# A hybrid attention and pooling layer: x loaded by tiles of tokens, scaled there and turned on TensorE, and the index queries projected in two lines

## The chip, the cores and the metric

The kernel runs on one core of one Trainium2 chip. The metric is device time in microseconds (us) of one execution; three executions of the kernel before took 515.8, 517.5 and 519.13 us, median 517.5. The core has five engines with a queue of instructions each, worked off in order: PE (TensorE, matrix products; PEld is its loading of stationary operands), DVE (VectorE), ACT (ScalarE), POOL (GpSimd) and SP, which here only issues transfers between main memory and SBUF.

## The reference, cut to what matters

One decoder layer for 1024 tokens of width 1024. The part that the change touches is the beginning:

```
mod = silu(c) @ w_ada + b_ada;  shift, scale, gate = split(mod, 3)
h = rms_norm(x, norm_w) * (1 + scale) + shift      # rms over a token's 1024 values
proj = h @ w_in                                    # w_in has 2888 columns
u_pool, g_pool, q, k, v, g_attn, qi, ki, wi = split(proj)
```

Behind it: a pooling mixer on `u_pool`; keys, queries and index queries with rotary positions; for every token the 256 keys with the best index score (computed from `qi`, `ki`, `wi`); attention over these; both branches gated and projected by `w_out`, times `gate`, added to x. Tokens below 256 take all their keys, so index queries are needed for tokens 256 to 1023 only.

## The kernel before, in words

All products are made with operands split in a high part (fp32r) and the rest: h is held as `hhi` and `hlo`, a weight as `wh` and `wl`, and a product is the three matmuls hhi·wh, hhi·wl, hlo·wh. h lies with its 1024 channels in 8 blocks j of 128 partitions and the tokens along the row.

The order of the instructions is not written out. Pieces of the work are generators ("strands") that yield operations; the class `Flow` (lines 302 to 402) keeps an estimated clock for each engine and, while the program is built, issues the operation that could start first, shifted by a number for each strand out of the table `EARLY` (line 38). `Either` (line 272) picks one of several engines for an operation in the same way. What results is a fixed queue for each engine. Every op is issued at line 228, so all rows of the profile carry L228.

**The lead** is what happens up to the first 61 us:

- `token_sums` (line 515) loads x transposed (`xT`, channels on partitions) in 8 blocks of 512 KB, the last two in halves, squares them on ACT, adds them on DVE, and sums over channels on PE by 48 one-column matmuls with a vector of ones. `token_scales` turns the 1024 roots into a row that is broadcast to all partitions (`rsb`).
- `modulations` (line 626) makes scale and shift of block j on DVE: two instructions over 128x1024, one for each of the two 512 KB tiles `wa` that `lead_loads` fetches; `gear` and `shift` finish the 128 values.
- `h_block` (line 687; `first_block` for j = 0): xn = x·rsb on POOL, then `hhi` and the shifted xn on ACT, and `hlo` on DVE or POOL, all over 1024 tokens.
- `query_loads` and `weight_splits` load the weights of the index queries (`wq`, four tiles of 512 KB in a ring `ld` of two) and split them, high part on ACT, rest on POOL.
- `lead_line` (line 737) projects the index queries for all 8 blocks j: for each j three products for tokens 512 to 1023 (4 matmuls of 512 columns each) and three for tokens 256 to 511 (4 of 256 columns), one after the other. It holds 6 of the 8 banks of PSUM, the other two hold silu(c), which `modulations` reads.

Then `main_line` begins: `key_value_rows` (the matmuls m<-wkh,hhi of 328 columns), gates, queries and the pooling mixer in the sequence `ORDER`, with the index scores, the selection and the attention on DVE, ACT and POOL beside it.

Of the kernel before, what the change touches and what calls it, by code (L numbers as in the profile page):

```python
# [7 lines left out]
F32 = mybir.dt.float32  # L8
F32R = mybir.dt.float32r
# [18 lines left out]
ORDER = "a0 a2 a1 q1 q2 | q0 m1 q3 m2 m3 m0 a3"  # L28
# [9 lines left out]
EARLY = {"main": 0.6, "fill": 0.4, "weights": 0.0, "evac": -1.0, "side": 0.2, "first": -0.4, "h": -0.2,  # L38
         "mods": -0.2, "select": -0.1, "scores": -0.6, "attend": -1.1, "late": 1.0, "kv": -0.3, "qi": -0.8,
         "pick": -0.6, "mix": -0.33, "rotated": 0.23, "query_loads": -0.28, "exps": -0.11, "score_sums": -1.07,  # L40
         "key_value_out": -0.93, "index_queries": -0.86, "norm": -0.46, "gate_loads": -1.2, "token_scales": -3.22,
         "gate_mods": -0.39, "unit": -1.06, "index_scores": -0.91, "lead_loads": 0.74, "out": -1.53,
         "lead_out": -1.24, "weight_loads": 0.51, "key_value_weights": 0.67, "main_line": 0.66, "output_line": 0.91,
         "turns": -1.46, "finish": -1.64, "index_keys": -1.47, "h_block": 0.28, "attention_keys": -0.36,
         "turned": -1.0, "h_blocks": -0.59, "gated": -2.15, "modulations": -0.09, "low": 0.65, "gear": -0.51,
         "attention": -0.86, "maxima": -0.99, "score_relus": -0.67, "gated 7": -1.82, "gated 3": -1.0,
# [5 lines left out]
         "exps 5": -0.25, "key_value_out 4": -3.2, "query_norms": 0.27, "exps 8": 0.04, "key_value_out 5": -1.22,  # L52
# [6 lines left out]
         "shift 6": -1.88, "key_value_out 6": -2.24, "norm 1": -2.54, "gear 4": 0.99, "products": -1.29,  # L59
         "shift 4": -0.32, "norm 5": -1.64, "low 1": -2.52, "turns 6": -2.43, "gated 6": -2.43, "turns 8": -1.76,  # L60
         "h_block 3": 0.04, "shift": 0.2, "gear 8": -2.5, "lead_line": 1.29, "gear 7": -1.58,
         "index_queries 3": -3.45, "index_queries 1": -2.08, "lead_splits": -0.3, "shift 5": -0.05,
         "first_block": -2.64, "shift 2": 0.74, "lead_out 1": -1.22, "shift 8": 1.3, "out 7": -0.3, "unit 3": -1.17,
         "turns 3": -2.02, "key_value_out 1": -2.25, "exps 4": -0.27, "mix 2": -0.25, "exps 2": 0.46, "out 6": -0.73,
         "gated 8": -2.42, "out 5": -1.79}
# [5 lines left out]
SAFE = {"side": 1.0, "unit": 0, "query_norms": 0, "h_block": 0.59, "rotated": 0.48, "query_loads": 0,  # L71
        "norm": 0.29, "weight_loads": 1.12, "key_value_out": 0.39, "turned": 0.26, "finish": 0, "index_keys": 0.85,
        "main_line": 0, "output_line": 0, "gate_mods": 1.06, "selection": 0, "low": 0.27, "maxima": 0,
        "attention": 0.44, "lead_out": 0, "score_relus": 0, "lead_loads": 0.28, "score_sums": 0.18, "mix": 0.96,
        "main": 0, "modulations": 0.09, "out": 0.39, "turns": 0.34, "exps": 0, "lead_line": 0.6, "shift": 0,
        "token_scales": 0.08, "index_scores": 0.19, "products": 0, "index_queries": 0.34, "attend": 0,
        "weight_splits": 0}

SCALED = (7,)

SUMS = (1, 4,)

WKM = 6
# [3 lines left out]
PHOP = -0.148  # L87
STT = 0.079
# [6 lines left out]
PW_POOL = 0.088  # L95
XO_POOL = 0.108
# [10 lines left out]
MIX = 4  # L107
# [6 lines left out]
WA_AHEAD = 3  # L114
# [13 lines left out]
class Op:  # L128
# [85 lines left out]
    def issue(self, flow):  # L214
# [8 lines left out]
        if self.eng == "ACT":  # L223
            table = TABLES.get(self.args[2] if len(self.args) > 2 else None)
            if table and table != flow.table:
                flow.table = table
                us += 1.3
        self.fn(*self.args, **self.kw)  # L228
# [180 lines left out]
def hybrid_layer(ctx, tc, xT, cT, nwT, badaT, wada, wq, wet, wkv, qnw, knw, wpool,  # L409
# [71 lines left out]
    ones = const([P, 1], F32)  # L481
# [32 lines left out]
    xt, hhi, hlo, wk = [], {}, {}, []  # L514
    tab = {}

    def token_sums():
# [3 lines left out]
        halves = [slice(512, 1024), slice(0, 512)]  # L521
        pieces = [(j, slice(0, 1024)) for j in range(6)] + [(j, c) for c in halves for j in (6, 7)]
        for j, c in pieces:
            if len(xt) == j:
                xt.append((yield big(s="xt")))
            yield SP.dma_start(xt[j][:, c], xT[j][:, c])
            if j == 0:
# [3 lines left out]
        yield G.memset(ones, 1.0)  # L531
# [19 lines left out]
        tab["sums"] = []  # L551
        for _ in range(2):
            tab["sums"].append((yield bank(4)))
        started = set()

        def sums(t, c, last):
            for h, half in enumerate(halves):
                if half.start >= c.start and half.stop <= c.stop:
                    for b in range(4):
                        o = half.start + b * P  # L560
                        yield mm(tab["sums"][h][:, b:b + 1], t[:, o:o + P], ones, h not in started, last and b == 3)
                        started.add(h)

        sq, acc = {}, None
        for j, c in pieces:
            if j not in sq:
                sq[j] = yield big(s="sq")
            yield A.activation(sq[j][:, c], xt[j][:, c], AF.Square)
            if j in SUMS:
                yield from sums(sq[j], c, False)  # L570
            elif acc is None:
                acc = sq[j]
                continue
            else:
                yield V.tensor_tensor(acc[:, c], acc[:, c], sq[j][:, c], op=OP.add)
                if j == NT - 1:
                    yield from sums(acc, c, True)
            if c.start == 0:
                flow.drop(sq[j])
        flow.drop(acc)  # L580

    def token_scales():
        rsb = yield big(s="rsb")
# [1041 lines left out]
```

## Time and profile before

| | us |
|---|---|
| three executions | 515.8, 519.13, 517.5 (median 517.5) |
| the profiled execution | 518.54, of which the span of the instructions is 516.8 |
| PE busy | 491.5 (95% of the span) |
| DVE, ACT, POOL busy | 417.1 (81%), 385.1 (75%), 149.5 (29%) |
| first matmul of the lead line | 23.51 |
| first matmul of the keys and values | 61.20 |

Times in the profile count from the start of the span. A group of the trace such as "43.59 1.09 PE ... x4" began at 43.59, and its four pipelined matmuls were busy for 1.09; what a group costs in a sequence is the distance to the start of the next one. "[0.83 <-DMA xt<-xT]" behind a row is the time that the engine sat idle before it, and what ended the wait.

### The profile page before, as it was taken

The numbers are of one execution on the slowest core, as the hardware profiler recorded it, in microseconds if no ns is written. First come the engines' busy times: TensorE is split into PE (matmuls) and PEld (weight loads), VectorE is DVE, ScalarE is ACT, GpSimd is POOL, SyncE is SP. The second block draws the span as 40 slices with busy tenths as digits, with TensorE's granted clock in tenths as the row PEclk, the third lists the DMA queues.
The fourth block names the chain that finished last, engine by engine and source line by source line (L and its number), as shares of the span: only waits on it lengthen the run. The fifth ranks groups of instructions, "written<-read, shape, count | busy, mean of one in ns | idle before, by whom it ended". The sixth has DMA issues, their size and how long they took to land.

```text
span 516.8 us, 8355 instructions
## 1 busy us (share of the span) xinstructions
PE 491.5 (95%) x2840; PEld 369.3 (71%) x2840; DVE 417.1 (81%) x890; ACT 385.1 (75%) x875; POOL 149.5 (29%) x166
## 2 busy tenths in 40 slices
PE   4899999999999989999999999999999999898996
PEld 4788899766768857878878776886664658453484
DVE  1799897799689799989999999778979995675342
ACT  6589433697778999999837999799898747669410
POOL 1399310001001133567033247524521222200000
PEclk9999999999999999999999998999999999999999
DMA  8996613011205112111120014575532135501054
GB/s 300 402 409 217 227 42 122 22 45 38 75 10 184 41 42 81 42 41 42 41 81 22 21 63 125 160 246 164 183 103 63 42 101 192 156 1 41 1 190 136
DMA packets 28171, 58.35 MB, mean 113 GB/s; under 512 B 3808, under 2 KB 7904, under 8 KB 28128
## 3 DMA queue, kind: packets, MB, share of 16 engines
q1 hardware_dynamic: 28128, 57.81, 33.2%
q8 instruction: 22, 0.36, 0.3%
q14 instruction: 21, 0.17, 0.1%
HBM read 47.32 MB, written 10.49 MB: 112 GB/s over the span
## 4 chain that ended last, share of the span: by engine, by line
PE 51%; DVE 24%; issue 7%; ACT 7%; POOL 4%; DMA 2%; DVEq 0%; SPq 0%; POOLq 0%; ACTq 0%
PE m L228 51%; DVE junk L228 7%; DVE selw L228 3%; ACT ex L228 3%; DVE ex L228 2%; POOL wl L228 1%; DVE nx L228 1%; DMA xo<-y_d 1%; DVE xq L228 1%; DVE wa L228 1%; ACT hhi L228 1%; DVE gp L228 1%; ACT ajunk L228 1%; DVE u L228 1%; POOL xn L228 1%
## 5 line engine op out<-in xcount | busy, mean ns | idle before, releaser
L228 PE MATMUL m<-hhi,wh 128*128 128x512 f32 (+1 forms) x320 | 120.9, 400 | 0.3 <-ACT hhi L228 0.3
L228 PE MATMUL m<-hhi,wl 128*128 128x512 f32 (+1 forms) x320 | 115.5, 383 | 0.0
L228 PE MATMUL m<-hlo,wh 128*128 128x512 f32 (+1 forms) x320 | 114.0, 381 | 0.5 <-DVE hlo L228 0.2
L228 ACT ACTIVATE ajunk<-key,xq 128x768 bf16<-128x768 uint16 (+2 forms) x93 | 96.3, 1036 | 1.3
L228 POOL TENSOR_TENSOR wl<-ld,wh 128x512 fp32r<-128x512 f32 x40 | 59.5, 1491 | 45.3 <-ACT wh L228 26.7
L228 PEld LDWEIGHTS m<-hhi,wh 128*128 128x128 f32 x320 | 59.7, 192 | 16.6 <-issue 4.1
L228 DVE TENSOR_SCALAR_CACHE_REDUCE junk<-key,xq 128x384 bf16<-128x384 uint16 (+2 forms) x93 | 69.1, 743 | 2.1
L228 PEld LDWEIGHTS m<-hhi,wl 128*128 128x128 f32 x320 | 59.6, 191 | 12.2 <-issue 1.4
L228 PEld LDWEIGHTS m<-hlo,wh 128*128 128x128 f32 x320 | 58.6, 188 | 13.0 <-DVE hlo L228 0.9
L228 ACT ACTIVATE ex<-ex,mx,c 128x384 f32<-128x384 f32 (+7 forms) x64 | 54.9, 859 | 5.1 <-DVE mx L228 5.0
L228 ACT ACTIVATE kt<-m 128x512 f32<-128x512 f32 (+1 forms) x80 | 37.7, 525 | 11.0 <-PE m L228 5.4
L228 DVE SCALAR_TENSOR_TENSOR score<-kt,c,score 128x1024 f32<-128x1024 f32 (+5 forms) x42 | 39.9, 951 | 7.3 <-ACT kt L228 5.5
L228 PE MATMUL m<-kT,qr 64*128 64x512 f32 (+3 forms) x192 | 40.6, 512 | 1.7 <-DVE mx L228 1.3
L228 DVE CUSTOM_DVE_ANT_0 ex<-m,key 128x512 f32<-128x512 f32 (+1 forms) x48 | 30.9, 662 | 7.2 <-PE m L228 7.0
L228 DVE SCALAR_TENSOR_TENSOR xo<-m,c,xo 128x512 f32<-128x512 f32 x23 | 17.2, 749 | 23.1 <-PE m L228 15.4
L228 PE MATMUL m<-pw,vrow 128*64 128x512 f32 x144 | 33.1, 599 | 0.1
L228 PEld LDWEIGHTS m<-kT,qr 64*128 64x128 f32 x192 | 19.4, 188 | 18.3 <-issue 11.0
L228 ACT CAST wh<-ld 128x512 fp32r<-128x512 f32 x33 | 20.3, 624 | 15.7 <-PE m L228 11.4
L228 POOL TENSOR_SCALAR_AFFINE_SELECT score<-score 128x128 f32<-128x128 f32 x6 | 3.8, 633 | 88.0 <-DVE score L228 80.8
L228 ACT COPY pw<-m 128x512 f32<-128x512 f32 x51 | 26.3, 610 | 3.9 <-PE m L228 3.9
L228 PEld LDWEIGHTS m<-c,ex 64*128 64x128 f32 x576 | 21.3, 139 | 10.0 <-ACT ex L228 3.2
L228 POOL TENSOR_SCALAR wh<-ld 128x512 fp32r<-128x512 f32 x23 | 17.7, 770 | 37.1 <-PE m L228 36.3
(193 smaller groups left out, 1062.5 us busy)
## 6 DMA issues: line engine op xcount, KB each, us to landing
wa<-wada SPq DMA_DIRECT2D x24, 512.0 KB, 7.5
ld<-wet SPq DMA_DIRECT2D x16, 512.0 KB, 3.4
ld<-wout SPq DMA_DIRECT2D x24, 256.0 KB, 3.0
xo<-xT SPq DMA_DIRECT2D x16, 256.0 KB, 3.8
y_d<-xo SPq DMA_DIRECT2D x16, 256.0 KB, 2.6
xo<-y_d SPq DMA_DIRECT2D x16, 256.0 KB, 3.0
outT<-xo SPq DMA_DIRECT2D x16, 256.0 KB, 2.3
xt<-xT SPq DMA_DIRECT2D x6, 512.0 KB, 7.3
```

Source lines behind the costliest of these rows:

```text
L228: self.fn(*self.args, **self.kw)
```

## The change

x is loaded with tokens on partitions (`xR`, 8 tiles of 128 tokens by 1024 channels), the tiles 7 to 4 (tokens 512 to 1023) first, and tiles 3 to 0 inside `lead_loads` before the `wa` tiles of block 2 (`XB = 2`). A token's sum of squares now comes along a row (`token_tile`: one instruction with accumulation on DVE or ACT), and its root scales the tile in place on DVE, POOL or ACT. `token_turns(n)` turns a half on PE: 64 transposes of 64 partitions by 128 channels for each half, in four groups q that fill two banks of PSUM each; `token_out` copies a bank to SBUF. The squares on PE, the sums on DVE and the row `rsb` are gone. `h_half` makes hhi and hlo for half a block (512 tokens). `lead_line` becomes two strands, one for tokens 512 to 1023 and one for 256 to 511, each over all 8 blocks; the weight chunks stay until both have used them. The loads of the key and value weights wait for the modulation of all 8 blocks (`WKM` 6 to 8), and `EARLY` has many new numbers. Behind the lead the work is the same; a few neighbours change places on DVE, POOL and PE, and q2 is projected before q1.

```diff
-ORDER = "a0 a2 a1 q1 q2 | q0 m1 q3 m2 m3 m0 a3"
+ORDER = "a0 a2 a1 q2 q1 | q0 m1 q3 m2 m3 m0 a3"
...
-         "gate_mods": -0.39, "unit": -1.06, "index_scores": -0.91, "lead_loads": 0.74, "out": -1.53,
+         "gate_mods": -0.39, "unit": -1.06, "index_scores": -0.91, "lead_loads": 1.12, "out": -1.01,
...
-WKM = 6
+COLD = 17.877
+
+XB = 2
+
+WKM = 8
...
+    def token_tile(st):
+
+        yield lambda: st in xr
+        t, r = xr[st], rs[:, st:st + 1]
+        sq = yield big(s="sq")
+        ways = [V.scalar_tensor_tensor(sq, t, 1.0, t, op0=OP.mult, op1=OP.mult, accum_out=r),
+                A.activation(sq, t, AF.Square, accum_out=r)]
+        yield Either(*ways) if st < 4 else ways[st == 4]
+        flow.drop(sq)
+        if st >= 4:
+            yield A.activation(r, r, AF.Sqrt, scale=1.0 / 1024.0, bias=eps_sb)
             yield V.reciprocal(r, r)
...
+                yield A.activation(rs[:, 0:4], rs[:, 0:4], AF.Sqrt, scale=1.0 / 1024.0, bias=eps_sb)
+                yield V.reciprocal(rs[:, 0:4], rs[:, 0:4])
+                rooted.append(st)
+            yield lambda: bool(rooted)
+        ways = [V.tensor_scalar(t, t, r, None, op0=OP.mult), G.tensor_scalar(t, t, r, 1.0, op0=OP.mult, op1=OP.mult),
+                A.activation(t, t, AF.Copy, scale=r)]
+        yield Either(*ways) if st < 4 else ways[st == 6]
+        token_scaled.append(st)
+
+    def token_turns(n):
+
+
+        toks = range(4 - 4 * n, 8 - 4 * n)
+        yield lambda: all(st in token_scaled for st in toks)
+        rows = slice(0, 64), slice(64, 128)
+        for q in range(NT // 2):
+            xt[q, n] = yield big(s="xt")
+            ps = []
+            for r in range(2):
+                ps.append((yield bank(keep=1 - r)))
+            yield Group([PE.transpose(ps[r][:, (j * 4 + b) * 64:(j * 4 + b + 1) * 64],
+                                      xr[st][rows[r], (2 * q + j) * P:(2 * q + j + 1) * P], ident[rows[r], rows[r]])
+                         for j in range(2) for b, st in enumerate(toks) for r in range(2)])
+            for r in range(2):
+                flow.spawn(token_out(q, n, r, ps[r]), "h")
+        flow.drop(*[xr[st] for st in toks])
...
     def lead_loads():
         for j in range(NT):
+            for st in (3, 2, 1, 0) if j == XB else ():
+                t = yield big(s="xr")
+                yield SP.dma_start(t, xR[st])
+                xr[st] = t
             yield lambda: len(modded) >= j - WA_AHEAD
...
+    def h_half(j, n, hi, lo):
+        c = halves[n]
+        x, g, m = xt[j // 2, n][:, j % 2 * 512:j % 2 * 512 + 512], gs[:, j:j + 1], mod_sb[:, j:j + 1]
+        yield Either(A.activation(hi[:, c], x, AF.Identity, scale=g, bias=m),
+                     V.tensor_scalar(hi[:, c], x, g, m, op0=OP.mult, op1=OP.add))
         hhi[j] = hi
...
+    def lead_line(c):
+        if c:
+            yield lambda: len(turned_in) == 2 * NT
+        p = (slice(512, 1024), slice(256, 512))[c]
```

In the rows below, xr_176, xr_173, xr_166 and xr_161 are the tiles of tokens 0 to 511, hhi_272 and hhi_293 are blocks 0 and 1, hhi_365 is block 2, hhi_401 block 3; c_76 is the identity matrix.

SP's queue around the second half of x, before (behind the last piece of x):

```order
L228 DMA wa_205<-wada 128x1024
L228 DMA wa_207<-wada 128x1024
L228 DMA ld_209<-wq 128x1024
L228 DMA wa_210<-wada 128x1024
L228 DMA wa_215<-wada 128x1024
L228 DMA wa_217<-wada 128x1024
L228 DMA wa_219<-wada 128x1024
```

and now (behind the first four tiles of x):

```order
L238 DMA wa_147<-wada 128x1024
L238 DMA wa_149<-wada 128x1024
L238 DMA ld_151<-wq 128x1024
L238 DMA wa_152<-wada 128x1024
L238 DMA wa_159<-wada 128x1024
L238 DMA xr_161<-xR 128x1024
L238 DMA xr_166<-xR 128x1024
L238 DMA xr_173<-xR 128x1024
L238 DMA xr_176<-xR 128x1024
L238 DMA wa_274<-wada 128x1024
```

Four tiles of x moved from ahead of the first `wa` to behind the `wa` of block 1; the last of them is the 13th transfer of 512 KB.

PE's queue in the lead, before, from the first block to the second:

```order
L228 MATMUL m<-hhi_253,wh_212 128x512 x4
L228 MATMUL m<-hhi_253,wl_213 128x512 x4
L228 MATMUL m<-hhi_253,wh_212 128x256 x4
L228 MATMUL m<-hhi_253,wl_213 128x256 x4
L228 MATMUL m<-hlo_254,wh_212 128x512 x4
L228 MATMUL m<-hlo_254,wh_212 128x256 x4
L228 MATMUL m<-hhi_302,wh_232 128x512 x4
```

and now, from the first product of the first block to the last of the second:

```order
L238 MATMUL m<-hhi_272,wh_154 128x512 x4
L238 MATMUL m<-hhi_272,wl_155 128x512 x4
L238 MATMUL m<-hlo_273,wh_154 128x512 x4
L238 MATMUL m<-hhi_293,wh_208 128x512 x4
L238 MATMUL m<-hhi_293,wl_209 128x512 x4
L238 MATMUL m<-c_76,xr_176 128x64 x2
L238 MATMUL m<-c_76,xr_173 128x64 x2
L238 MATMUL m<-c_76,xr_166 128x64 x2
L238 MATMUL m<-c_76,xr_161 128x64 x2
L238 MATMUL m<-c_76,xr_176 128x64 x2
L238 MATMUL m<-c_76,xr_173 128x64 x2
L238 MATMUL m<-c_76,xr_166 128x64 x2
```

Only five groups of matmuls stand ahead of the transposes of the second half; the products of blocks 2 to 7, the third product of block 1 and all products of 256 columns stand behind the first of them.

ACT's queue in the same place, now (sq are squares, xt the copies of turned x out of PSUM):

```order
L238 ACTIVATE sq_180,c_92<-xr_176 128x1024
L238 ACTIVATE c_92<-c_92,c_79 128x4
L238 ACTIVATE xr_161<-xr_161,c_92 128x1024
L238 ACTIVATE xr_166<-xr_166,c_92 128x1024
L238 CAST wh_280<-ld_278 128x512
L238 COPY xt_323<-m 128x8x64
L238 CAST wh_359<-ld_278 128x512
L238 COPY xt_323<-m 128x8x64
L238 ACTIVATE hhi_365<-xt_206,c_88,c_89 128x512
L238 COPY xt_351<-m 128x8x64
L238 ACTIVATE hhi_272<-xt_323,c_88,c_89 128x512
L238 ACTIVATE hhi_293<-xt_323,c_88,c_89 128x512
```

The copies that free PSUM for the next transposes stand in one queue with casts of weights and with the hhi of blocks 0 to 2.

## Rows read from the trace of the kernel before

**Rows 1.** The page's first part: busy us, share of the span, instructions of each engine.
```profile
PE 491.5 (95%) x2840; PEld 369.3 (71%) x2840; DVE 417.1 (81%) x890; ACT 385.1 (75%) x875; POOL 149.5 (29%) x166
```

**Rows 2.** Busy time by stretch: stretch, length, PE, PEld, DVE, ACT, POOL, clock, DMA share, GB/s.
```profile
100.00:120.00 20.00, 20.00 (x119) 13.98 (x118) 18.39 (x21) 18.01 (x33) 0.33 (x1) 1.00 0.16 54
```

**Rows 3.** Timeline of PE in the lead: start, busy us, what.
```profile
23.51 2.06 PE L228 MATMUL m<-hhi,wh 128*128 128x512 f32 x4
25.37 1.91 PE L228 MATMUL m<-hhi,wl 128*128 128x512 f32 x4
...
43.59 1.09 PE L228 MATMUL m<-hhi,wh 128*128 128x512 f32 x4
...
45.45 0.63 PE L228 MATMUL m<-hhi,wh 128*128 128x256 f32 x4
...
46.40 1.56 PE L228 MATMUL m<-hlo,wh 128*128 128x512 f32 x8
47.80 1.09 PE L228 MATMUL m<-hhi,wh 128*128 128x512 f32 x4
...
56.61 0.40 PE L228 MATMUL m<-hhi,wh 128*128 128x512 f32 x1
...
61.20 0.32 PE L228 MATMUL m<-wkh,hhi 128*128 128x328 f32 x1
```

**Rows 4.** Timeline of ACT where it waits for transfers of 512 KB.
```profile
7.80 1.06 ACT L228 ACTIVATE sq<-xt 128x1024 f32<-128x1024 f32 x1 [0.83 <-DMA xt<-xT]
...
19.66 1.14 ACT L228 CAST wh<-ld 128x512 fp32r<-128x512 f32 x2 [0.58 <-DMA ld<-wq]
```

**Rows 5.** Groups of instructions by shape: count, busy us, mean ns of one, idle before.
```profile
L228 DVE SCALAR_TENSOR_TENSOR wa<-wa,m 128x1024 f32<-128x1024 f32 x16 | 18.9, 1210 | 0.0
L228 ACT ACTIVATE sq<-xt 128x1024 f32<-128x1024 f32 x6 | 6.3, 1053 | 1.8 <-DMA xt<-xT 1.8
L228 ACT ACTIVATION_READ_ACCUMULATOR ajunk<-key,xq 128x1 f32 x93 | 17.5, 188 | 0.0
L228 ACT ACTIVATE c<-m,c 128x4 f32<-128x4 f32 x2 | 0.5, 254 | 2.5 <-PE m L228 2.5
L228 DVE RECIPROCAL c<-c 128x4 f32<-128x4 f32 x2 | 0.3, 174 | 0.9 <-ACT c L228 0.9
L228 ACT ACTIVATE hhi<-xn,c 128x1024 fp32r<-128x1024 f32 x1 | 1.2, 1152 | 0.0
L228 ACT ACTIVATE hhi<-xn,c 128x512 fp32r<-128x512 f32 x2 | 1.4, 722 | 1.1 <-DVE xn L228 0.8 <-DVE c L228 0.3
L228 ACT CAST wh<-ld 128x512 fp32r<-128x512 f32 x8 | 4.8, 607 | 0.6 <-DMA ld<-wq 0.6
L228 ACT COPY rsb<-m 128x512 f32<-128x512 f32 x2 | 1.2, 577 | 0.0
L228 POOL TENSOR_SCALAR wh<-ld 128x512 fp32r<-128x512 f32 x23 | 17.7, 770 | 37.1 <-PE m L228 36.3
```

**Rows 6.** Instructions on tile ld in the first 65 us: ns min/median/max, first and last start.
```profile
L228 POOL TENSOR_TENSOR wl<-ld,wh x8: 1270/1787/2284, 20.4 to 50.4; 128x512 fp32r<-128x512 f32 x8
```

**Rows 7.** Timeline of PE, transposes of 64 partitions late in the span, and what follows.
```profile
478.71 2.83 PE L228 MATMUL m<-c,ex 64*128 64x64 f32 x80
481.47 7.09 PE L228 MATMUL m<-pw,vrow 128*64 128x512 f32 x32
```

**Rows 8.** Busy time in a stretch with two waits of PE, columns as in Rows 2.
```profile
190.00:195.00 5.00, 3.76 (x10) 1.38 (x11) 4.93 (x11) 4.93 (x14) 1.27 (x1) 0.71 0.01 2
```

**Rows 9.** Timeline of PE in that stretch.
```profile
190.29 0.39 PE L228 MATMUL m<-qsh,c 128*8 128x512 f32 x1 [0.75 <-DVE qsh L228]
191.63 0.39 PE L228 MATMUL m<-qsl,c 128*8 128x512 f32 x1 [0.95 <-POOL qsl L228]
...
192.55 0.63 PE L228 MATMUL m<-qsh,c 128*8 128x512 f32 x1
192.98 0.63 PE L228 MATMUL m<-qsl,c 128*8 128x512 f32 x1
```

More of the change, by code (lines that the diff above doesn't have):

```diff
@@ L59 @@
[L59 to L63, printed above, removed]
@@ L64 @@
-         "turns 3": -2.02, "key_value_out 1": -2.25, "exps 4": -0.27, "mix 2": -0.25, "exps 2": 0.46, "out 6": -0.73,
-         "gated 8": -2.42, "out 5": -1.79}
[5 rows of a table added]
+         "exps 5": -0.25, "key_value_out 4": -3.2, "query_norms": 0.27, "exps 8": -0.52, "key_value_out 5": -1.22,
[6 rows of a table added]
+         "key_value_out 6": -2.24, "norm 1": -2.54, "gear 4": -1.05, "products": -1.29, "shift 4": -0.32,
+         "norm 5": -1.64, "low 1": -2.52, "turns 6": -1.25, "gated 6": -2.43, "turns 8": -1.76, "h_block 3": -0.55,
@@ L105 @@
 GM = 4
-MIX = 4
+MIX = 5
 KEEP = 7
@@ L227, in issue @@
                 us += 1.3
+        if self.eng == "PE" and t < COLD:
+            us = 2 * us
         self.fn(*self.args, **self.kw)
@@ L511, in modulation, with constants @@
         flow.drop(w)
-    xt, hhi, hlo, wk = [], {}, {}, []
+    xr, xt, hhi, hlo, wk = {}, {}, {}, {}, []
     tab = {}
-    def token_sums():
+    halves = slice(512, 1024), slice(0, 512)
+    squared, rooted, token_scaled, turned_in = [], [], [], []
+    def constants():
         yield G.memset(ident, 1.0)
@@ L549, in token_sums @@
         tab["scp"] = psum[:, 0:1024]
[L551 to L579, printed above, removed]
@@ L691, in hybrid_layer @@
[L691 to L714 removed]
+        flow.spawn(h_half(j, 0, hi, lo), "h")
@@ L747, in lead_line @@
+    def lead_line(c):
+        if c:
+            yield lambda: len(turned_in) == 2 * NT
+        p = (slice(512, 1024), slice(256, 512))[c]
+        n = p.stop - p.start
+        for j in range(NT):
+            yield lambda: len(chunks) > j
+            whi, wlo = chunks[j]
+            turns = [(k, range(4)) for k in (0, 1, 2)] if j < NT - 1 else [(k, (e,)) for e in range(4) for k in (0, 1, 2)]
+            for k, es in turns:
                 yield lambda: (j, c) in (lo_in if k == 2 else hi_in)
@@ L748, in lead_line @@
                 for e in es:
[L749 removed]
+                    if (e, c) not in lead_acc:
                         if c == 0:
[L751 removed]
+                            lead_acc[e, c] = yield bank()
                         else:
[L753 to L756 removed]
@@ L765, in lead_line @@
-            flow.drop(whi, wlo)
-        flow.spawn(main_line(), "main")
-    def lead_out(e, acc):
-        x = yield big(w=768, s="qix")
-        for c, o in ((0, 256), (1, 0)):
-            n = 512 - 256 * c
-            yield A.copy(x[:, o:o + n], acc[e, c][:, :n])
-            if c == 0 or e % 2:
-                flow.drop(acc[e, c])
+                            pair = lead_acc[e - 1, c] if e % 2 else (yield bank())
+                            lead_acc[e, c] = pair
+                ops = []
@@ new lines, in lead_line @@
+                for e in es:
+                    o = e % 2 * 256 if c else 0
+                    wt, ht = ((whi, hhi[j]), (wlo, hhi[j]), (whi, hlo.get(j)))[k]
+                    ops.append(mm(lead_acc[e, c][:, o:o + n], wt[:, e * P:(e + 1) * P], ht[:, p],
+                                  j == 0 and k == 0 and (c == 0 or e % 2 == 0),
+                                  j == NT - 1 and k == 2 and (c == 0 or e % 2 == 1)))
+                yield Group(ops)
+                if j == NT - 1 and k == 2:
+                    lead_ends.append((es[0], c))
@@ new lines, in lead_line, with lead_out @@
+            lead_used.append(j)
+            if lead_used.count(j) == 2:
+                flow.drop(whi, wlo)
+        if len(lead_used) == 2 * NT:
+            flow.spawn(main_line(), "main")
+    lead_copied = []
+    def lead_out(e):
+        yield lambda: (e, 0) in lead_ends
+        x = yield big(w=768, s="qix")
+        yield A.copy(x[:, 256:768], lead_acc[e, 0])
+        flow.drop(lead_acc[e, 0])
+        yield lambda: (e | 1, 1) in lead_ends
+        yield A.copy(x[:, 0:256], lead_acc[e, 1][:, e % 2 * 256:e % 2 * 256 + 256])
+        lead_copied.append(e)
+        if e ^ 1 in lead_copied:
+            flow.drop(lead_acc[e, 1])
@@ L1504, in output_line @@
         yield from project_attended(1)
-    flow.now(token_sums())
-    flow.spawn(token_scales(), "h")
+    flow.now(constants())
+    for st in range(NT - 1, -1, -1):
+        flow.spawn(token_tile(st), "h")
+    for n in range(2):
+        flow.spawn(token_turns(n), "h")
     flow.spawn(query_loads(), "weights")
@@ L1510, in hybrid_layer @@
     flow.spawn(modulations(), "mods")
-    flow.spawn(h_blocks(), "h")
+    for j in range(NT):
+        flow.spawn(h_block(j), "h")
     flow.spawn(key_value_weights(), "kv")
@@ L1514, in hybrid_layer @@
     flow.spawn(lead_splits(), "weights")
-    flow.spawn(lead_line(), "main")
+    for c in range(2):
+        flow.spawn(lead_line(c), "main")
+    for e in range(4):
+        flow.spawn(lead_out(e), "evac")
     flow.spawn(gate_mods(), "late")
```

170 lines of the change are left out of this document (54 added, 116 removed), and 28 rows, old and new, of the table EARLY.

## The prediction, made before the changed kernel ran

> **What bounds the kernel now.** I read the shares of the engines first: PE is busy for 491.5 of 516.8 us [rows 1]. That says little by itself, since busy PE need not be useful PE, so I then took busy time by stretches: behind the lead PE has no gap at all for a long time (20.00 of 20.00 us in the stretch shown [rows 2]), while DVE and ACT have some. So whenever the keys and values start sooner or later, everything behind them moves with them, one for one. The change works on the time ahead of that point: the first matmul of the keys and values starts at 61.20 [rows 3].
>
> PE's timeline in the lead splits those 61.20 us. The lead line's first group starts at 23.51, and the next at 25.37: 1.86 us for four matmuls of 512 columns. Later such a group costs half: two of them from 43.59 to 45.45, 0.93 each; two groups of 256 columns take 45.45 to 46.40, 0.475 each; a block of six groups takes 43.59 to 47.80, 4.21 us, and the last block 56.61 to 61.20, 4.59 [rows 3]. So the lead line is 7 x 4.21 + 4.59 = **34.1 us** of PE at full rate. Measured it took 37.7: 3.6 us were lost to the half-rate start and to waits. Only a lead that starts PE's *continuous* run before 61.2 - 34.1 = 27.1 us wins anything.
>
> **The change part by part.** My sum is against the profiled execution, 518.54 us with a span of 516.8; the median shown is 517.5, 1.0 lower, and I apply the difference that I find to the median.
>
> *Transfers.* The second tile of 512 KB lands at 7.80, the eleventh (eight tiles of x, two wa, one ld) at 19.66 [rows 4]: 1.32 us each, the queue never dry. By the new order of SP the fourth tile lands at 10.4, the ld of block 0 (7th) at 14.4, the first tile of the second half of x (10th) at 18.4, its last (13th) at 22.3, the ld of blocks 2 and 3 (16th) at 26.3. The bytes are the same.
>
> *First half.* Tile 4: a square with accumulation (1.05 + 0.19), root 0.25, reciprocal 0.17, scaling about 1: ready at 10.4 + 2.9 = 13.3. On ACT two casts of ld stand ahead of the copies of turned x: 14.4 + 2 x 0.61 + 4 x 0.58 = 17.9, then hhi of block 0: the first group of the lead line can start at 18.5 [rows 4, 5], **5 us earlier** than 23.51. Block 1 needs two wa instructions on DVE (1.21 each [rows 5]) behind those of block 0. The five groups ahead of the second half's transposes are 5 x 0.93 = 4.65 us of work and end near 24.6, also if they run at half rate in part.
>
> *The new wait.* Behind these five groups PE's queue holds the transposes of the second half, and every other product stands behind them. They need all four tiles scaled. ACT takes the four squares from 18.8 (it finishes a copy first): 4 x 1.24 and one copy of 0.58 end at 24.3; root and reciprocal 24.9; then two tiles are scaled on ACT (I take 1.15 each, from the row of 1024 columns [rows 5]) and two on POOL beside it (0.77 for 512 columns; between 0.77 and 1.54 for 1024, I take 1.2), both done at **27.3**. PE idles from 24.6 to 27.3. The early start is thus worth 4.65 us of work done, not 5 us of time.
>
> *PE's work from 27.3 on.* 34.1 - 4.65 = 29.4 of products, plus 64 transposes of this half at 2.83/80 = 0.035 each, the only row of such transposes [rows 7], 2.3 us. The 64 of the first half lie in time in which PE only waited before; the 48 one-column matmuls that they replace lay there too. 27.3 + 29.4 + 2.3 = **59.0**, 2.2 us ahead of 61.2, if PE never waits again.
>
> *But it waits for PSUM.* Silu(c) and four accumulators leave two banks, and each of the four groups q of transposes fills two; the next q waits until both copies are out. ACT's queue from 27.2: cast 0.61, copy 0.58, cast 0.61, copy 0.58: the second q starts at 29.7, while PE finished the first q and hlo of block 1 at 28.9: 0.8 lost. hhi of block 2 (0.72) holds the next group until 30.4: nearly nothing. Then copy, two hhi of 0.72, a shift of about 0.3, and two copies stand on ACT before the fourth q, which starts at 33.9; PE had its work done at 32.8: 1.1 lost. A scaling of 0.72 between the last two copies holds the first group of 256 columns by 0.2. Sum 2.1: lead end **61.1**. Fewer than 2.1 would take copies faster than 0.58, which no row shows.
>
> *The clock.* After two waits of 0.75 and 0.95 us with one matmul between them, the granted clock of that stretch was 0.71, PE partly at the lower of its levels, 1.2 instead of 2.4 GHz, and single matmuls of 512 columns started 0.43 apart [rows 8, 9]. The new wait of 2.7 us is longer than those together, so part of the transposes, hlo of block 1 and the first group of block 2 may run at half rate. Bounds: nothing (all hidden in the waits for copies) to 2.4 us (the transposes ahead of the last, and two groups, at twice their price, less the 0.8 and 0.2 of waits that they fill). I take 1.0, nearer to nothing, because PE waits there for ACT in any case. Lead end **62.1**, which is 0.9 later than 61.20.
>
> The Trainium skill ("TensorE: Matmul & The Clock Gate", Part 4: PE-mode transpose) says that transposes do not count as work for PE's clock. By that rule the stretch from 24.6 to 34 would have few groups that keep the clock up, and the loss would be the full 2.4 instead of 1.0, a time of 519.8. The trace speaks for the milder value: 80 transposes in a row take 0.035 each, and the 32 matmuls of 512 columns behind them 0.22 each [rows 7], full rate.
>
> *Everything else at nothing, with its cover.* DVE from 25 on: 12 wa instructions of 1.21 and some 20 small or half-width ones of about 0.5 end near 50, before PE needs the last block; if that cover goes, block 7 is late. The key and value weights load behind the last wa: 28 tiles end at 42, four table tiles and the weights by about 53, split by 57, under the lead's end at 62; with a lead ending at 57 they would be the next thing late. q2 before q1, and the neighbours that change places later, are the same work; the waits of [rows 9] stand in the same queues as before.
>
> Sum: +0.9 on 517.5, **518.4 us**. No change that can be measured (about 1%, 5.2 us, is what a measurement here can tell from none).
>
> **The rivals.**
>
> *Faster: the waits vanish.* If the copies or the clock cost nothing, the lead ends at 59.0, 2.2 early: 515.3. If also the squares of the second half were no backlog on ACT (23.5 instead of 24.3, the last tile landing at 22.3 plus 1.24) 514.5. For more, something behind the lead has to help: the two waits at 189 to 192 with the half rate behind them cost 1.7 and about 7 x 0.2 for the rest of that stretch, 3.1 us [rows 8, 9]; without them too, 511.4. For it: the change starts PE 5 us sooner, and the late queue orders are touched. Against: PE's remaining work at 27.3 is a sum of rows, and only 2.2 us are in it. Chance 0.2, of which 0.12 for over 1%.
>
> *Slower: POOL becomes the bound.* After 27.3 POOL has 13 tensor-tensor instructions of 512 columns (four with weights of blocks 4 to 7, on which PE waits directly) and 5 scalings of 0.77. The former took 1.27 to 2.28 each in this same stretch, median 1.79 [rows 6]. At 1.79: 27.3 + 23.3 + 3.9 + 1.0 of waits = 55.5, and behind the last weight split PE still has about a block, 4.6: 60.1, hidden. It decides from 1.95 on: 27.3 + 13 x 1.95 + 3.9 + 1.0 + 4.6 = 62.1. At 2.28 the lead ends at 66.4: **+5.2, 522.7**. For it: DVE now has scalings from SBUF to SBUF beside POOL's, and a long POOL instruction is one that stood beside DVE work. The Trainium skill ("SBUF — State Buffer", on the shared port pair) says that one of the two blocks the other for a whole instruction; the trace agrees with its spread of 1.27 to 2.28. Against: POOL had the same load before (6 xn of 1024 and 8 splits) and did not stop PE for more than tenths. Chance 0.2, of which 0.14 for over 1%, where it adds to a clock that stays low.
>
> **How the numbers follow.** Forecast case (lead end 59.5 to 64.5, +-1 behind it) 0.6: its own range is 515 to 522. Faster rival 0.2, slower rival 0.2. The likeliest is 518.4. For 8 in 10 I cut both rivals at half: **513 to 523**. Faster by over 1%: 0.12 from the first rival and 0.02 for luck behind the lead: 0.14. Slower by over 1%: 0.14 and 0.02: 0.16. Within 1%: 0.70.
>
> **What would show it.** In the changed profile: first lead matmul of 512 columns near 18.5; a gap of PE of 2 to 4 us ending near 27 in front of the transposes of xr; short waits of PE for ACT's xt between 28 and 37; no large gap behind that; first matmul of the keys and values at 61 to 64. It would be wrong if the transposes of the second half start before 25.5 (then the gain is real), if the group price is not 0.93 there, if PE waits for POOL's wl after 40, or if the start of the keys and values moves and the end does not move with it.

## The result and the profile after: 1.4% faster, most of it behind the lead

The changed kernel took 510.99 us (median of four executions, 509.85 to 511.8) where the kernel before took 517.65 (515.8 to 519.13) on the same chip: ratio 0.9861, 95% interval 0.9837 to 0.9885, 6.7 us less. The forecast of 518.4 was wrong, and 511.0 lies below its range of 513 to 523. The same kernel on another chip, beside later experiments, gave 0.9876 (0.9856 to 0.9897) and 511.39.

The profiled execution took 511.55 us with a span of 509.7, 7.1 less than the span of 516.8 before. The page's first part, against [rows 1]:

```profile
PE 482.0 (95%) x2912; PEld 361.2 (71%) x2912; DVE 417.9 (82%) x910; ACT 381.8 (75%) x879; POOL 152.0 (30%) x182
```

PE's timeline in the lead, against [rows 3] (start, busy us, what, idle before it and what ended that):

```profile
12.82 3.58 PE L238 MATMUL m<-c,xr 64*128 64x64 f32 x64 [5.92 <-DVE xr L238]
17.07 0.98 PE L238 MATMUL m<-hhi,wh 128*128 128x512 f32 x3 [0.68 <-DVE hhi L238]
19.04 0.73 PE L238 MATMUL m<-hhi,wh 128*128 128x512 f32 x1 [0.99 <-ACT xt L238]
19.56 1.91 PE L238 MATMUL m<-hhi,wl 128*128 128x512 f32 x4
...
23.71 1.07 PE L238 MATMUL m<-hhi,wl 128*128 128x512 f32 x4
25.27 0.72 PE L238 MATMUL m<-c,xr 64*128 64x64 f32 x16 [0.49 <-POOL xr L238]
25.92 1.20 PE L238 MATMUL m<-hlo,wh 128*128 128x512 f32 x4
27.04 0.27 PE L238 MATMUL m<-c,xr 64*128 64x64 f32 x1
27.68 0.71 PE L238 MATMUL m<-c,xr 64*128 64x64 f32 x15 [0.36 <-ACT xt L238]
...
30.32 0.70 PE L238 MATMUL m<-c,xr 64*128 64x64 f32 x15 [0.54 <-DVE xt L238]
...
59.11 0.32 PE L238 MATMUL m<-wkh,hhi 128*128 128x328 f32 x1
```

The lead line starts at 17.07, runs its first groups at half rate (granted clock 0.50 from 20 to 22 us; a group of four takes 1.91 us, later 1.07), waits only 0.49 for the second half of x, and then waits 0.36 and 0.54 for copies of turned tiles. The keys and values start at 59.11 instead of 61.20: the lead gave **2.1** of the 7.1 us.

Where the rest came from shows when the k-th instruction of a form on PE is paired with the k-th of the same form before. The pairs start 2.1 us earlier from 61 to 160 us, still 2.0 at 300, then 4.1 at 330 to 360, 4.8 at 385, 2.9 at 400, 3.3 at 410 to 435, 5.1 at 445 to 470 and 6.05 from 480 to PE's end. The last 1.0 is behind the last row of DVE, which in the kernel before and in the changed one reads

```profile
511.89 0.75 DVE L228 SCALAR_TENSOR_TENSOR xo<-m,c,xo 128x512 f32<-128x512 f32 x1 [1.97 <-PE m L228]
```

```profile
505.83 0.75 DVE L238 SCALAR_TENSOR_TENSOR xo<-m,c,xo 128x512 f32<-128x512 f32 x1 [1.97 <-PE m L238]
```

to the end of the span, 4.2 and 3.1 us: the last write. So 5 us of this pair came from places that the prediction had costed at nothing. PE's waits behind 62 us, first of the kernel before, then of the changed one (us in total, times, longest; seven and six other lines are left out):

```profile
PE m L228 <- ACT ex L228: 2.1, 2, 1.3
PE m L228 <- DVE mx L228: 1.7, 5, 0.5
PE m L228 <- ACT st L228: 1.7, 2, 0.9
...
PE m L228 <- ACT pw L228: 0.8, 2, 0.4
```

```profile
PE m L238 <- DVE mx L238: 2.7, 5, 1.4
PE m L238 <- DVE mpl L238: 1.4, 1, 1.4
PE m L238 <- ACT ex L238: 1.3, 2, 0.8
...
PE m L238 <- ACT st L238: 0.4, 1, 0.4
```

The waits for `st` nearly go, those for `ex` shrink, and `mx` and `mpl` take part of it back. The sums are 10.5 and 9.8, so waits give 0.7 of the 5. The granted clock is another part. In the two first profiles it fell to half near 190 us, in both, and at these places:

```profile
300.00:330.00 30.00, 28.73 (x120) 21.17 (x119) 27.43 (x90) 25.88 (x65) 15.14 (x15) 0.89 0.33 104
```

```profile
390.00:420.00 30.00, 29.46 (x211) 16.54 (x212) 26.14 (x69) 19.83 (x41) 7.59 (x9) 0.94 0.23 71
```

(columns as in [rows 2]; kernel before, then the changed one; each at 1.00 in the other's stretch). Half of the time at half rate, counted behind the lead, is 5.1 us in the kernel before and 3.4 in the changed one, 1.7 less. Waits, clock and last write make 3.4; the other 1.6 is time in which PE is busy at full clock, though the matmuls behind the lead are the same 2584. Whether the half rate belongs to a kernel or to an execution, one profile of each can't say.

### The profile page after: what moved, and what is told of

It is laid out like the page before. It is cut to its first block, busy times and chain, and to the rows that moved or that the text cites. A ratio compares the mean times of both kernels' runs of the same rounds, so it can differ in the third digit from the quotient of the medians.

```text
span 509.7 us, 8516 instructions
## 1 busy us (share of the span) xinstructions
PE 482.0 (95%) x2912; PEld 361.2 (71%) x2912; DVE 417.9 (82%) x910; ACT 381.8 (75%) x879; POOL 152.0 (30%) x182
## 4 chain that ended last, share of the span: by engine, by line
PE 82%; DVE 8%; DMA 5%; ACT 3%; issue 1%; POOL 0%; SPq 0%; DVEq 0%
PE m L238 82%; DMA wa<-wada 4%; DVE ex L238 3%; ACT ex L238 2%; DVE junk L238 1%; DMA xr<-xR 1%; DVE selw L238 1%; DVE mpl L238 0%; DVE wa L238 0%; DVE mx L238 0%; DVE xq L238 0%; DVE xo L238 0%; DVE gp L238 0%; DVE st L238 0%; POOL qsl L238 0%
## 5 line engine op out<-in xcount | busy, mean ns | idle before, releaser
L238 PE MATMUL m<-hlo,wh 128*128 128x512 f32 (+1 forms) x320 | 115.2, 383 | 0.0
L238 ACT CAST wh<-ld 128x512 fp32r<-128x512 f32 x31 | 19.2, 624 | 23.8 <-DMA ld<-wout 7.5
L238 PE MATMUL m<-c,ex 64*128 64x64 f32 x576 | 24.0, 226 | 3.8 <-DVE mx L238 1.8
```

## The experiments

All were timed against the kernel before on their own chip. "Lost to the clock" is (1 - mean granted clock) x time, averaged over the executions; over 88 executions of the kernel before it is 4.2 us. It is a measure and not a price, since half rate ahead of a wait can be hidden.

**1. Lead and later order apart.** The new and old numbers can be mixed so that each engine's queue is that of one kernel up to about 60 us and that of the other behind it. The edit of the changed kernel, with a few numbers picked out of its long table (the other mixture has the reverse in the kernel before):

```diff
-ORDER = "a0 a2 a1 q2 q1 | q0 m1 q3 m2 m3 m0 a3"
+ORDER = "a0 a2 a1 q1 q2 | q0 m1 q3 m2 m3 m0 a3"
-MIX = 5
+MIX = 4
-         "norm 3": -0.05, "norm 8": 0.01, "weight_loads": 0.77, "output_line": 1.13, ...
+         "norm 3": -3.08, "norm 8": -2.88, "weight_loads": 0.51, "output_line": 0.91, ...
```

> The lead of the changed kernel with the order behind the lead of the kernel before (the numbers of the strands that start after the keys and values, MIX, PHOP, STT, PW_POOL, XO_POOL and q1 before q2 are the old ones; rows on every engine up to about 60 us are those of the changed kernel, behind it those of the kernel before). Keys and values start near 59.1 in each theory. Theory A (two parts: the lead gives what its start gives, 2.1 us, and the new order behind it the other 4.6): 517.6 - 2.1 = 515.5. Theory B (the lead gives all, the later order is worth nothing, as the prediction costed it): 511.0, and the 4.6 us show in places behind 300 us without any change of order there. Theory C (the lead's 2.1 us are swallowed by waits behind it, the late order gives all): 517.6.

Measured 514.87 (ratio 0.9939, 0.9919 to 0.9959), 2.9 less; lost to the clock 4.5. One profile places this only roughly, because the start of the keys and values differs between executions: 60.95 to 61.86 in nine profiles with the old lead, 59.11 to 60.22 in six with the new one, and 61.89 in the profile of this kernel, whose execution took 517.15.

> The lead of the kernel before with the order behind the lead of the changed kernel. Keys and values start near 61.2. Theory A (two parts that add): 517.6 - 4.6 = 513.0. Theory B (the lead gives all): 517.6. Theory C (the late order gives all): 511.0. If the two parts add, this gain and that of the new lead with the old late order sum to 6.6.

Measured 512.9 (0.9894, 0.9877 to 0.9911), **4.9 less**; lost to the clock 2.05. Two parts that about add (7.8 against 6.7): the lead gives some six tenths of what the order behind it gives. The second theory, by which the later order is worth nothing, falls, and the prediction stood on that.

**2. Is PE's start behind the lead passed on?**

```diff
+MORE = 9
...
+                        for _ in range(MORE):
+                            nc.tensor.matmul(ps_all, lhsT=hhi[0][:, 0:P], rhs=hhi[0][:, 0:512], start=True, stop=True)
+                        first(*a, **k)
```

> The changed kernel with nine more matmuls of 512 columns on PE in front of the first matmul of the keys and values (their result is overwritten), 9 x 0.227 = 2.04 us of PE work at that one place, and no other row moved on any engine. One for one, as the prediction has it: keys and values start at 61.15, the end is 2.0 later, 511.0 + 2.0 = 513.0. Rival: the waits of PE behind the lead (9.3 us in all in the changed kernel) are on engines that don't move with it and take up part of the delay: 511.0 to 512.0.

Measured 513.12 (0.9906, 0.989 to 0.9922), 2.1 more than 510.99 and 1.7 more than the later 511.39: about one for one. In its profile PE's rows are 2.92 later than in the first profile of the changed kernel where the keys and values start (62.03; the lead itself was 0.9 later), and still 2.85 later at 385 us, so the waits between take up nothing. At 391 the first profile fell to half rate and this one did not; from there the rows are 1.2 later. The prediction's first paragraph stands; what it did not say is that the order behind can change by itself.

**3. What bounds the lead?**

```diff
+WARM = (14, 3)
...
+                nc.tensor.matmul(ps[:, 0:P], lhsT=ident, rhs=ident, start=True, stop=True)
...
+            if q + n == 0:
+                warmed(ops[0], ps[0], WARM[0])
...
+                if j + k + c == 0:
+                    warmed(ops[0], lead_acc[0, 0], WARM[1])
```

> The changed kernel with 14 one-tile fp32 matmuls on PE between the broadcast of silu(c) and the first turned tiles of x, where PE idles from 6.9 to 12.8, and 3 more in front of the first group of the lead line (results overwritten); no other row moved. It is to keep PE busy before the first group, so that the stretch with the granted clock at 0.5 (18.8 to 22.2) may fall away. Theory A (that half rate is hidden: what follows it waits for the second half of x, scaled at 25.1, in any case): first turned tiles of the second half stay at 25.3, keys and values at 59.1, 511.0. Rival (the half rate is on the path): the five groups in front of the second half end 1.7 earlier and the lead with them, 509.3.

Measured 510.74 (0.9871, 0.9849 to 0.9893): nothing. Its PE timeline:

```profile
19.63 1.09 PE L240 MATMUL m<-hhi,wl 128*128 128x512 f32 x4
...
22.37 1.07 PE L240 MATMUL m<-hhi,wl 128*128 128x512 f32 x4
26.40 0.71 PE L240 MATMUL m<-c,xr 64*128 64x64 f32 x16 [2.96 <-POOL xr L240]
```

The half rate is gone (1.09 instead of 1.91), and the wait for xr is 2.96 instead of 0.49: here half rate in front of a wait was hidden. Now the readiness itself, less and (with a copy in place issued ahead, `first_doubled`) more:

```diff
+        if st < 4:
+            for op in ways:
+                op.fn = first_left_out(op)
         yield Either(*ways) if st < 4 else ways[st == 6]
```

> The changed kernel without the first scaling of xr of the second half on ACT and the first on POOL (two of the four tiles of the earlier half of the tokens stay unscaled, so that part of the computation is left out); no other row moves. The second half of x is then ready 1.1 us earlier. Theory A (its readiness sets the lead's end): PE waited in front of its transposes 0.5 us in the first profile of the changed kernel and 0.9 to 3.0 in the three later ones with its lead, so keys and values start 0.5 to 1.1 earlier: 509.9 to 510.5. Rival (the PSUM copies behind it, or other work, bound the lead): 511.0.

Measured 511.03 (0.9884, 0.9863 to 0.9906): nothing.

> The changed kernel with one more pass over a tile of xr (a copy in place, 1024 columns) on ACT and one on POOL ahead of the scalings of the second half; no other row moves, values stay the same. The second half is ready 1.1 us later. Theory A (its readiness sets the lead's end, one for one): 512.1, and up to 1.7 more in executions where the longer wait of PE is followed by half rate, so 512.1 to 513.8. Rival (hidden, since other work bounds the lead): 511.0.

Measured 511.57 (0.9878, 0.9855 to 0.9901), 0.2 to 0.6 more than the changed kernel's 511.39 and 510.99: between the theories and within what can't be told from nothing. Next, both edits at once, with the changed kernel beside it.

> The changed kernel itself once more, on the chip of the three kernels run with it, as their reference and for a second profile: 511.0 by all theories. Its lead: turned tiles of the second half start between 25.3 and 26.4 and keys and values 33.8 us later if no half rate falls behind that start (33.8 in the profiles of the changed kernel, of the delayed and of the warmed one), up to 1.7 later if it does.

Measured 511.39; turned tiles at 26.09, keys and values at 59.9, 33.8 apart as expected.

> The changed kernel with both edits that by themselves moved nothing: the seventeen extra matmuls that keep PE at full rate ahead of the second half, and two of the four scalings of the second half left out. Theory A (two things bound the start of the turned tiles at once, PE's own groups at half rate and the readiness of the second half, so that taking one away shows the other): with both away they start near 24.9, keys and values 33.8 later at 58.7, that is 0.4 to 1.4 earlier than with either edit (59.85 and 60.2 in their profiles): 509.6 to 510.4. Rival (the copies of the turned tiles out of PSUM, or the load of blocks 2 and 3, which a cast awaited until 25.9 in the profile with two scalings less, bound the lead): 511.0.

Measured 513.18 (0.9899, 0.9882 to 0.9915): no gain. Keys and values start at 60.0, as in the unedited kernel beside it (59.9), so for the lead the rival holds; the end came 1.8 later than that kernel's, which neither theory has, and why, I don't know (in its profile the clock is 0.94 from 300 to 330). The lead shows what took over; ACT, and then PE:

```profile
26.18 0.62 ACT L240 CAST wh<-ld 128x512 fp32r<-128x512 f32 x1 [0.98 <-DMA ld<-wq]
```

```profile
25.29 0.71 PE L240 MATMUL m<-c,xr 64*128 64x64 f32 x16 [1.37 <-POOL xr L569]
...
27.33 0.27 PE L240 MATMUL m<-c,xr 64*128 64x64 f32 x1 [0.20 <-ACT xt L240]
28.34 0.71 PE L240 MATMUL m<-c,xr 64*128 64x64 f32 x15 [0.73 <-ACT xt L240]
```

The turned tiles start 0.8 earlier, but the copies that PE needs next stand on ACT behind a cast that waits for a transfer until 26.18, and PE pays 0.93 there, 0.35 in the unedited kernel. Three things end within 1 us of each other: PE's first groups, the scaled half, and the weights of blocks 2 and 3. Each covers the others.

```diff
-XB = 2
+XB = 3
```

> The changed kernel with XB = 3: the four tiles of the earlier half of the tokens are issued one block of loads later (two wa and one ld, 3 x 1.27 = 3.8 us); eight groups instead of five then stand on PE ahead of the turned tiles of that half, and the order behind the lead is unchanged. Theory A (PE's wait in front of the turned tiles is what the lead pays): ready 3.8 later, covered by 3 x 0.93 = 2.8 of groups, so keys and values 1.0 later: 512.0, and up to 1.7 more where half rate follows the wait. Rival (the copies behind and PE's work are the bound, the place of the loads has slack): 511.0.

Measured 512.87 (0.9904, 0.9885 to 0.9922), 1.5 over the 511.39 beside it; keys and values at 62.0. The direction of theory A holds; the price came from a place that I had not named, PE waiting 2.59 for hhi of block 1 at 23.91, because two casts, which waited 1.27 for their transfer, and a square now stand ahead of it on ACT.

**4. What in the later order?** First the attention's numbers and all the rest apart, on the old lead.

```diff
-"norm 2": -0.66, "norm 3": -3.08, "norm 8": -2.88, "turns 3": -2.02, "exps 8": 0.04, "gate_loads": -1.2, ...
+"norm 2": -0.51, "norm 3": -0.05, "norm 8": 0.01, "turns 3": -3.11, "exps 8": -0.52, "gate_loads": -1.94, ...
```

> The kernel before with the new numbers of the attention strands alone (exps, norm, turns, gated, gate_loads, products): on PE six rows of mph move past a group of turned ex and three groups of turned st stand later; rows on the engines move only behind 340 us. Of the 4.9 us that the whole new order behind the lead gave (512.9 against 517.8), theory A puts to these rows the waits that became shorter there: PE for ACT st (1.7 us in the kernel before, 0.4 after), ACT ex (2.1, 1.3) and ACT pw (0.8, 0.4), 2.5 us in sum, less 1.0 us more for DVE mx: 516 to 515.5. Rival: the half rate near 318 us went with these rows too: 513.

Measured 515.02 (0.9945, 0.9925 to 0.9966), 2.65 less: theory A's side, not the rival's 513, and in its profile the clock from 300 to 330 is still 0.94.

> The kernel before with all other numbers of the order behind the lead new (out, out_line, mix, rotated, weight_loads, PHOP, STT, MIX, PW_POOL, XO_POOL, q2 before q1), the attention strands with the old ones: on PE only the products of u move, on DVE, ACT, POOL and SP rows between 80 and 330 us. Theory A: the half rate near 318 us (granted clock 0.89 from 300 to 330 in both profiles with the old order, 1.00 in the four with the new one) goes with these rows, 2 to 3.4 us less: 514.4 to 515.8, and with the attention numbers' part the sum is 4.9. Rival: that half rate is an accident of the execution and these rows are worth nothing: 517.8.

Measured 515.15 (0.9966, 0.9952 to 0.998), 2.5 less by the medians, 1.8 by the ratio. The time is in theory A's range, but the clock from 300 to 330 is 0.94 here too, so its cause is not shown. Then single sets of numbers:

> The kernel before with three new numbers alone (norm 2, norm 3, norm 8): on PE two groups of four turned st stand later, one behind eight groups of turned ex and its scores, one behind four; nothing else moves on PE. Theory A: PE's waits for st at 409 (0.76 us) and 441 (0.94 us) shrink or go, as they did in the changed kernel (0.39 and none): 517.7 - 1.3 = 516.4. Rival: what PE doesn't wait for there it waits for at the next row (DVE mx, ACT ex): 517.7.

Measured 515.43 (0.9953, 0.9935 to 0.9971), **2.7 less by three numbers** (2.4 by the ratio), more than theory A's 1.3. Lost to the clock 3.0 instead of 4.4 on this chip, and the median of time x clock falls by 1.2 (513.9 to 512.7): about half of the gain is time at equal clock, and half is that PE ran at half rate for less of the time. The 1.2 is the size that theory A gave, but not by its cause. PE's waits for `st` shrink from 1.7 and 1.9 in two profiles of the kernel before to 0.9, and those for `mx` grow from 1.7 to 2.7,

```profile
PE m L195 <- DVE mx L195: 2.7, 5, 1.3
...
PE m L195 <- ACT st L195: 0.9, 2, 0.5
```

as the rival has it; all waits together are 11.1, against 10.5 and 11.3. What got shorter is busy time of PE at full clock, 433.5 us behind the lead against 435.1 and 435.2. From start to start, without waits and half rate, 1.1 of that lies in the 96 matmuls m<-kT,qr of 512 columns, 22.5 instead of 23.6, with other neighbours than before; no run takes this apart further.

> The kernel before with the new numbers of weight_loads, main_line and output_line alone: loads and stores of the last 200 us are issued in another order on SP, and some finishing rows of DVE, ACT and POOL move behind 380 us. Theory A: 517.8. Theory B (spread): 516.8. Theory C (PE's waits at 441 us, 0.94 for st of ACT, go with the finishing rows, as in the run with the new middle part, which won 0.7 us there): 515.2 to 516.8.

Measured 515.16 (0.9957, 0.9941 to 0.9973), 2.2 less by the ratio and 3.1 by the medians: theory C. The two others, and the kernel before again:

> The kernel before with the pool mixer's new numbers alone (MIX 5 instead of 4, mix 2, rotated 1, query_norms): on PE the products of u come somewhat later, on DVE and POOL rows between 150 and 330 us move. Theory A (the middle part's gain is here, since its PE rows are the only ones of PE that the middle part moves, and the half rate near 318 follows them): 515.2. Theory B (it is spread): 516.8. Theory C (it is in the late loads): 517.8.

Measured 517.42 (0.9997, 0.9981 to 1.0013): nothing.

> The kernel before with the new numbers of the strands out alone: rows of DVE, ACT and POOL between 80 and 190 us move, none of PE, and PE has hardly a gap there (127.2 busy of 128 us from 62 to 190). Theory A and C: 517.8. Theory B (spread): 516.8.

Measured 518.39 (1.0002, 0.9984 to 1.0021): nothing, as theories A and C have it.

> The kernel before once more, for a second profile and as a measure of what two equal kernels differ by: ratio 1.000 within 0.002. Theory A (half rate near 318 us goes with the old order): granted clock about 0.89 from 300 to 330 again. Rival (an accident of the execution): 1.00 or 0.94 there. The end after the last instruction of VectorE: 3.1 us if the first profile's 4.2 was that execution's, 4.2 if it is the kernel's.

Measured 518.5 (1.0005, 0.9986 to 1.0024). Its clock from 300 to 330 is 1.00, so theory A falls as it stands: the kernel does not run at half rate there in every execution, and in this one that stretch lies at 476 instead. But the order has a hand in it. Of nine profiles with the old later order or a part of it, seven have half rate at 318 to 321 us and six at 473 to 478; of nine with the whole new one, one and none. The end behind DVE's last row is 4.2 again, but 3.0 to 3.3 in six of the seven other profiles with the old order or a part of it, so the old order alone does not fix it; what does, no run shows.

The second profiles of the two kernels, paired like the first, lie 1.9 apart up to 360 us, 2.8 at 430, 4.4 at 450 and 6.6 from 480. The step near 440 is in both pairs, the one near 320 only in the first.

What the loads' numbers did near 440 us shows in two profiles. The kernel before in its second one, DVE, ACT and PE:

```profile
438.78 0.75 DVE L228 SCALAR_TENSOR_TENSOR xo<-m,c,xo 128x512 f32<-128x512 f32 x1 [2.03 <-DMA xo<-y_d]
439.44 0.19 DVE L228 RECIPROCAL sume<-sume 128x8 f32<-128x8 f32 x1
```

```profile
439.73 0.62 ACT L228 COPY st<-sume 128x512 f32<-128x512 f32 x1 [2.89 <-DVE sume L228]
```

```profile
440.39 0.66 PE L228 MATMUL m<-c,st 128*128 128x128 f32 x4 [1.15 <-ACT st L228]
```

and with the new loads' numbers:

```profile
436.63 0.75 DVE L195 SCALAR_TENSOR_TENSOR xo<-m,c,xo 128x512 f32<-128x512 f32 x1 [2.42 <-PE m L195]
437.30 0.20 DVE L195 RECIPROCAL sume<-sume 128x8 f32<-128x8 f32 x1
```

```profile
438.26 0.66 PE L195 MATMUL m<-c,st 128*128 128x128 f32 x4
```

A finishing row of DVE stood waiting for a load that SP issued at 432.71, behind a load of weights, and that landed at 438.33; a reciprocal of eight columns stood behind it, ACT's copy behind that, and PE behind the copy for 1.15 us. With the load issued ahead of the weights (at 431.21, landed at 436.54) PE doesn't wait. PE's rows are 1.04 earlier at 430 and 2.60 at 450, so this place gives about 1.5 of the 2.2 to 3.1. All waits together are 11.0 against 11.3, since others grew or came up.

## Why the prediction was wrong, by its own steps

**"Everything else at nothing, with its cover"** is the step that failed: "the same work" was taken to mean the same time. The whole later order is worth 4.9 us. Two of its sets of numbers, norm (2.4 to 2.7) and the late loads (2.2 to 3.1), would add up to all of it, though the two alone were never built together, and two (mixer, out) give nothing. With the new lead and the old order behind it, the time is 514.87, inside the range. What the order changed shows when PE's time from the first matmul of the keys and values to PE's end is split (us, from the profiles; the last column is half of the time at half rate):

| | idle | busy | of it lost at half rate |
|---|---|---|---|
| kernel before, two profiles | 10.5, 11.3 | 440.2, 438.6 | 5.1, 3.4 |
| new lead, old order | 10.0 | 439.6 | 5.1 |
| old lead, new order | 10.8 | 435.6 | 1.7 |
| changed kernel, two profiles | 9.8, 9.9 | 436.9, 435.4 | 3.4, 1.7 |

PE's waits were in the profile before, and the prediction priced only the two of [rows 9], which did not move: qsl 1.0 and qsh 0.8 are the same after. But waits are the small part. They go from one row to the next, and their sum is 10.0 to 11.3 with the old order and 9.8 to 10.8 with the new. Busy time falls by about 3.5, by less half rate and by 0.6 to 1.8 at full clock (434.5 to 435.2 with the old order, 433.5 to 433.9 with the new). The one place where a chain of waits is shown to have been worth its time is the load behind the wait for `st` near 440.

**The gap before the second half, 27.3.** Off by 2.0, and with the 1.0 for the clock this is the lead's whole miss (62.1 predicted, 59.11 measured): the turned tiles start at 25.27, which the prediction named as the sign that the gain is real. I had ACT's four squares end at 24.3 behind a backlog; they kept pace with the transfers, and these were quicker (1.27 instead of 1.32 us each). ACT's rows:

```profile
17.36 1.06 ACT L238 ACTIVATE sq<-xr 128x1024 f32<-128x1024 f32 x1 [0.27 <-DMA xr<-xR]
...
21.20 1.06 ACT L238 ACTIVATE sq<-xr 128x1024 f32<-128x1024 f32 x1
...
22.93 2.19 ACT L238 ACTIVATE xr<-xr,c 128x1024 f32<-128x1024 f32 x2 [0.25 <-DVE c L238]
```

In four later profiles with the same scalings the tiles started at 26.1 to 26.4, so 0.8 to 1.1 of these 2.0 belongs to the first profile's chip or execution.

**From there to the keys and values: 33.8 predicted (27.3 to 61.1), 33.84 measured**, with parts that traded: copies cost 0.90 instead of 2.1 (DVE took some of them), the products 0.4 less, and turning 1.6 more than 2.3, since the 64 turns stand in four pieces and each change between them and the products costs PE some tenths (a group between two pieces takes 25.92 to 27.04, 1.12, not 0.93).

**The clock, 1.0.** In the first profile nothing behind the gap and half rate ahead of it, where it is hidden. The bounds, 0 to 2.4, held: in the run with the new lead and the old order the wait of 2.09 was followed by half rate,

```profile
26.42 0.71 PE L203 MATMUL m<-c,xr 64*128 64x64 f32 x16 [2.09 <-POOL xr L203]
...
29.87 2.07 PE L203 MATMUL m<-hhi,wh 128*128 128x512 f32 x4
31.87 1.11 PE L203 MATMUL m<-c,xr 64*128 64x64 f32 x16
32.91 2.07 PE L203 MATMUL m<-hhi,wl 128*128 128x512 f32 x4
```

a group took 2.07 instead of 1.19 (granted clock 0.50 from 30 to 34 us), and the keys and values started at 61.89, 35.5 behind the first turned tiles instead of 33.8: 1.65 lost. In the other seven profiles with this lead nothing was lost there, also behind the longer wait of 2.96. The Trainium skill ("TensorE: Matmul & The Clock Gate", Part 4: PE-mode transpose) says that transposes don't count as work for the clock. The loss of 2.4 that I drew from it came in none of the eight. Ahead of the gap the profiles agree with it: of the six without extra matmuls there, five ran groups behind the first 64 turned tiles at half rate (by the price of a group; in one of the five, the delayed kernel, the granted clock reads 1.00 there), and the two with seventeen fp32 matmuls around them did not. They don't prove it, since these matmuls also cut PE's idle time before the tiles, from 5.92 to 2.63.

**One for one**: right (2.04 put in, 2.1 measured). **The rivals**: POOL was no bound; its products on the weights took 1.27 to 1.41 in the lead, where I feared up to 2.28. The faster rival had the sign right and, at 511.4, the size of its far end, but by another cause: it wanted the waits at 189 to 192 gone, and they stayed.

Open: why the new order, and the norm numbers alone, leave PE less time at half rate and shorten its busy time at full clock, and why the two lead edits together ended 1.8 later with the same start of the keys and values.

## What to carry to other kernels

A row that only changes places is not free when PE stands behind it: list PE's waits in the profile before, and look which of the moved rows release them, also through two other engines and a load. Then add up PE's idle and busy time before and after by themselves: here the waits mostly moved on to the next row, and more of the gain was in the clock and in busy time. Before pricing a wait in a lead, look for the next thing that ends within a microsecond of it: here three did, and taking away one or two of them moved nothing. Separate an early change from a late one by building both mixtures; their results add up here within about 1 us (2.9 and 4.9 against 6.7).

## What the runs showed of the hardware

Executions of one kernel differ by where PE falls to half rate: near 318 us for 6.8 us in one profile of the kernel before, and not there but at 476 in the next. The mean granted clock of its 88 executions gives a loss of 4.2 us; with the new later order on the same lead it was 2.05. So a change of 1% can lie nearly half in the clock, and a single pair of profiles can put it at the wrong place.

Half rate costs less than its length where a wait follows. With the new loads' numbers PE kept full rate behind the waits near 192 us, where the second profile of the kernel before fell to half; its rows gained 1.6 there and lost 1.0 of it again by 240, when PE waited 0.7 for DVE's u, a wait that the other profile does not have.
